# The last unit's second half loaded as one 32 KB part instead of two 16 KB parts

## The chip, the cores and the metric

The kernel runs on one core of a Trainium2 chip. The metric is the device time in microseconds (us), the median of several runs. Before the change it was 780.93 us (780.90 to 780.98, three runs). A profile covers a span that is 1.8 us shorter than the time of the run that it was taken in (779.3 against 781.07 for the kernel before). A transfer is issued by an engine's instruction (SyncE's, for nearly all of those told of here) and waits in that engine's queue for the 16 DMA engines, which carry it in packets; it has landed when the last of the 16 has reported its share.

## The reference

For each of 32 x 128 rows there are four rows of 4096 logits (heads) and four prior logits. Each head goes through a softmax, and the four results are added with the softmax of the priors as weights.

```python
prior_probs = np.exp(prior - prior.max(axis=-1, keepdims=True))
prior_probs = prior_probs / prior_probs.sum(axis=-1, keepdims=True)
softmax = np.exp(logits - logits.max(axis=-1, keepdims=True))
softmax = softmax / softmax.sum(axis=-1, keepdims=True)
mixture = np.sum(prior_probs[..., None] * softmax, axis=2)
```

268.4 MB of logits are read and 67.1 MB are written.

## The kernel before

The rows are cut into 32 units of 128 rows, one row per partition. A unit's four heads are 16 KB each per partition, 2 MB each in all. A tile of two units' logits (`ltile`) is loaded by SyncE's DMA queue; unit u goes into the place of unit u - 2.

```python
def load(u):
    if u == 0 or u >= U - 3:
        cuts = (0, 2, 3, 4) if u == U - 1 else (0, 2, 4)
    else:
        cuts = (0, H)
    for h, to in zip(cuts, cuts[1:]):
        ld = nc.sync.dma_start(
            out=ltile[:, u % 2, h:to], in_=lg[u // J, u % J, :, h:to, :]
        )
        if u >= 2:
            only(ld, adds[u - 2, 0] if h == 0 else exps[u - 2, to - 1])
        else:
            only(ld)
        for k in range(h, to):
            loads[u, k] = ld
```

`only(ins, *keep)` says that the instruction waits for those named and for nothing else. So the part with heads h to `to` waits until unit u - 2 is done with that place, and a head's exponential waits for the load that its head came in.

The loop does, per head, an exponential with a running sum on ScalarE, and then, for all four heads together or, in the last four units, for two at a time (`m` = 4 or 2), a reciprocal on VectorE, a product on GpSimd and the weighted adds on VectorE. The last add of the last unit is done in two halves, each followed by its own store:

```python
for h in range(H):
    ...
    exp(h, *((stores[u - 4],) if late else ()))
    if (h + 1) % m:
        continue
    g = h + 1 - m
    mul = weigh(g, m, *(free if g == 0 else ()))
    for k in range(g, h + 1):
        n = 2 if u == U - 1 and k == H - 1 else 1
        w = V // n
        for c in range(n):
            add(k, mul, c * w, (c + 1) * w)
            if n > 1:
                store(u, acc, nc.sync, c * w, (c + 1) * w)
```

The stores of units 28 to 31 go out on SyncE's queue too, behind the last loads.

The softmax here doesn't subtract the row's maximum and nothing guards it: scores larger than these inputs give would overflow.

## Time and profile before

| what | before | how to read it |
|---|---|---|
| time | 780.93 us | median |
| span of the profile | 779.3 us | first to last instruction of the trace |
| DMA engines | over 90% busy in 39 of 40 slices | the bound |
| VectorE, ScalarE | 67%, 60% busy | not the bound |
| last part of unit 31 lands | 758.96 us | from the trace's landing records |
| half stores of unit 31 issued | 771.19 and 773.45 us | from SyncE's instructions |
| last landing | 778.37 us | 0.91 us before the end of the span |

The lines behind this are shown in the prediction, where they are read. From the list of DMA issues, for the second half store alone (its size, and us from issue to landing):

```profile
out_dram<-ltile SPq DMA_DIRECT2D x1, 1024.0 KB, 4.9
```

### The profile page before, as it was taken

The page shows a single profiled execution, that of the slowest core. Times are in us where ns is not written, and L with a number is a line of the kernel's source. Part 1 is how long each engine was busy: PE and PEld are TensorE (multiplying, and loading weights), DVE is VectorE, ACT ScalarE, POOL GpSimd, SP SyncE. Part 2 cuts the span into 40 slices and gives each one's busy share as a digit, 9 for nine tenths or more (in the row PEclk, how much of TensorE's full clock was granted, in tenths as well). Part 3 has the DMA queues.
Part 4 walks back from the last instruction along what each step waited for, and adds up shares of the span by engine and source line. Part 5 has one row for each costly group of instructions (what it writes and reads, how often), then busy time and mean ns, then how long its engine had stood idle before and what let it go on. Part 6 is the DMA issues. An engine that isn't in the chain of part 4 may idle for free.

```text
span 779.3 us, 654 instructions
## 1 busy us (share of the span) xinstructions
DVE 521.0 (67%) x174; ACT 466.7 (60%) x258; POOL 8.3 (1%) x41
## 2 busy tenths in 40 slices
DVE  4447875558755587555775557855578655689886
ACT  4476555775457755577555675546765567657782
POOL 0000000000000000000000000000000000000000
DMA  9999999999999999999999999999999999999998
GB/s 407 457 417 401 470 407 434 428 461 428 405 467 403 458 420 433 442 443 418 431 454 407 454 408 467 420 415 447 432 442 417 463 399 463 410 427 433 434 429 377
DMA packets 10117, 335.66 MB, mean 431 GB/s; under 512 B 1136, under 2 KB 1136, under 8 KB 1152
## 3 DMA queue, kind: packets, MB, share of 16 engines
q1 hardware_dynamic: 6048, 276.83, 82.3%
q10 hardware_dynamic: 4064, 58.79, 17.6%
q14 instruction: 5, 0.04, 0.0%
HBM read 268.50 MB, written 67.11 MB: 431 GB/s over the span
## 4 chain that ended last, share of the span: by engine, by line
DMA 64%; ACT 27%; DVE 6%; issue 2%; POOL 0%; DVEq 0%; POOLq 0%
DMA ltile<-in_logits_dram 62%; ACT ebuf L159 19%; ACT ltile L159 8%; DVE obuf L177 5%; DMA out_dram<-obuf 2%; DVE ltile L183 1%; POOL coeff L170 0%; DVE rden L168 0%; DVEq L240 0%; POOLq L240 0%; POOLq L170 0%
## 5 line engine op out<-in xcount | busy, mean ns | idle before, releaser
L183 DVE SCALAR_TENSOR_TENSOR obuf<-ebuf,coeff,obuf 128x4096 f32<-128x4096 f32 x90 | 403.6, 4484 | 3.8 <-POOL coeff L170 0.6
L159 ACT ACTIVATE ebuf<-ltile 128x4096 f32<-128x4096 f32 x90 | 322.9, 3589 | 7.4 <-DMA ltile<-in_logits_dram 7.4
L159 ACT ACTIVATE ltile<-ltile 128x4096 f32<-128x4096 f32 x38 | 137.3, 3614 | 280.6 <-DMA ltile<-in_logits_dram 280.6
L168 DVE RECIPROCAL rden<-dsum 128x4 f32<-128x4 f32 (+1 forms) x36 | 6.3, 175 | 227.9 <-ACT ebuf L159 225.1
L177 DVE TENSOR_SCALAR obuf<-ltile,coeff 128x4096 f32<-128x4096 f32 x30 | 70.6, 2353 | 10.2 <-POOL coeff L170 10.2
L183 DVE SCALAR_TENSOR_TENSOR ltile<-ltile,coeff 128x4096 f32<-128x4096 f32 (+1 forms) x7 | 27.0, 3875 | 0.8 <-POOL coeff L170 0.6
L159 ACT ACTIVATION_READ_ACCUMULATOR ebuf<-ltile 128x1 f32 x90 | 16.8, 186 | 0.0
L170 POOL TENSOR_TENSOR coeff<-rden,pp 128x4 f32<-128x4 f32 (+1 forms) x36 | 7.2, 200 | 755.3 <-DVE rden L168 745.4
L159 ACT ACTIVATION_READ_ACCUMULATOR ltile<-ltile 128x1 f32 x38 | 7.1, 186 | 0.0
L139 DVE TENSOR_REDUCE pmax<-pr 16x256 f32<-16x1024 f32 x1 | 1.2, 1208 | 7.8 <-DMA pr<-in_prior_dram 7.8
L141 ACT ACTIVATE pr<-pr 16x1024 f32<-16x1024 f32 x1 | 1.1, 1055 | 7.8 <-DVE pr L140 7.8
L177 DVE TENSOR_SCALAR ltile<-ltile,coeff 128x4096 f32<-128x4096 f32 x2 | 4.7, 2354 | 0.6 <-POOL coeff L170 0.6
L144 DVE TENSOR_TENSOR pn<-pr,pmax 16x1024 f32<-16x1024 f32 x1 | 1.9, 1939 | 0.1
L141 ACT ACT_TABLE_LOAD x1 | 1.3, 1283 | 1.2 <-PEq L229 1.2
L142 DVE TENSOR_REDUCE pmax<-pr 16x256 f32<-16x1024 f32 x1 | 1.2, 1207 | 1.1 <-ACT pr L141 1.1
L149 DVE STREAM_TRANSPOSE pp<-pn 32x256 f32<-32x256 f32 x4 | 1.7, 435 | 0.1
L143 DVE RECIPROCAL pmax<-pmax 16x256 f32<-16x256 f32 x1 | 1.7, 1741 | 0.0
L140 DVE TENSOR_TENSOR pr<-pr,pmax 16x1024 f32<-16x1024 f32 x1 | 1.2, 1211 | 0.0
L138 POOL MEMSET pn<- 32x1024 f32 x1 | 0.9, 941 | 0.3 <-POOLq L229 0.3
L229 POOL MEMSET const-bfloat16-1.0<- 128x1 bf16 x1 | 0.1, 106 | 0.0
L229 POOL MEMSET const-uint8-127<- 128x1 uint8 x1 | 0.1, 106 | 0.0
L229 POOL MEMSET const-float32-0.0<- 128x1 f32 x1 | 0.1, 103 | 0.2 <-issue 0.2
(1 smaller groups left out, 0.1 us busy)
## 6 DMA issues: line engine op xcount, KB each, us to landing
out_dram<-obuf ACTq DMA_DIRECT2D x28, 2048.0 KB, 29.4
ltile<-in_logits_dram SPq DMA_DIRECT2D x7, 4096.0 KB, 26.1
ltile<-in_logits_dram SPq DMA_DIRECT2D x2, 2048.0 KB, 30.9
out_dram<-obuf SPq DMA_DIRECT2D x2, 2048.0 KB, 33.9
out_dram<-ltile SPq DMA_DIRECT2D x1, 2048.0 KB, 17.2
out_dram<-ltile SPq DMA_DIRECT2D x2, 1024.0 KB, 4.8
ltile<-in_logits_dram SPq DMA_DIRECT2D x28, 30.9
pr<-in_prior_dram ACTq DMA_DIRECT2D x1, 64.0 KB, 7.0
```

The costliest lines, as they stand in the source:

```text
L139: nc.vector.reduce_max(pmax, pr, axis=AX.X)
L140: nc.vector.tensor_sub(pr, pr, pmax.unsqueeze(2).to_broadcast([G, R, H]))
L141: nc.scalar.activation(pr, pr, AF.Exp)
L142: nc.vector.reduce_sum(pmax, pr, axis=AX.X)
L143: nc.vector.reciprocal(pmax, pmax)
L144: nc.vector.tensor_mul(pn[0:G].rearrange("g h r -> g r h"), pr, pmax.unsqueeze(2).to_broadcast([G, R, H]))
L149: nc.vector.transpose(pp[32 * t : 32 * (t + 1)], pq[:, :, :, 32 * t : 32 * (t + 1)])
L159: ex = nc.scalar.activation(es[h], lt[:, h], AF.Exp, accum_out=dsum[:, u, h : h + 1])
L168: rc = nc.vector.reciprocal(rden[:, u, h : h + n], dsum[:, u, h : h + n])
L170: mul = nc.gpsimd.tensor_mul(coeff[:, u, h : h + n], rden[:, u, h : h + n], ppu[:, h : h + n])
L177: st = nc.vector.tensor_scalar(out=acc[:, lo:hi], in0=es[h][:, lo:hi], scalar1=coeff[:, u, h : h + 1], scalar2=None, op0=ALU.mult,)
L183: st = nc.vector.scalar_tensor_tensor(out=acc[:, lo:hi], in0=es[h][:, lo:hi], scalar=coeff[:, u, h : h + 1], in1=acc[:, lo:hi], op0=ALU.mu ...
```

## The change

The intent: one DMA fewer, with larger pieces. Head 2 and head 3 of the last unit come as one part.

```diff
     def load(u):
         if u == 0 or u >= U - 3:
-            cuts = (0, 2, 3, 4) if u == U - 1 else (0, 2, 4)
+            cuts = (0, 2, 4)
         else:
             cuts = (0, H)
```

## The prediction

> **What bounds the kernel now.** I read the page first: the busy table, the strip of 40 slices and the chain shares.
>
> ```profile
> span 779.3 us, 654 instructions
> DVE 521.0 (67%) x174; ACT 466.7 (60%) x258; POOL 8.3 (1%) x41
> ...
> DMA  9999999999999999999999999999999999999998
> ...
> DMA 64%; ACT 27%; DVE 6%; issue 2%; POOL 0%; DVEq 0%; POOLq 0%
> ```
>
> VectorE and ScalarE are each busy for only about two thirds of the span, while the 16 DMA engines are over 90% busy in all slices but the last. 335.66 MB at the page's mean of 431 GB/s is 779 us, the whole span. So the kernel is bound by bytes moved, and the change moves none fewer. What it can change is only whether the DMA engines have work in every moment; since it touches the last unit alone, I looked at the end. (A unit is 128 rows; a head of it is 16 KB per row, 2 MB in all.) The table by stretches of time, with columns stretch, its length, busy VectorE, ScalarE and GpSimd, clock, DMA share, GB/s:
>
> ```profile
> 700.00:749.20 49.20, 41.35 (x18) 37.05 (x22) 1.18 (x6) 1.00 1.00 431
> 749.20:759.00 9.80, 9.22 (x4) 9.78 (x5) 0.20 (x1) 1.00 1.01 431
> 759.00:771.20 12.20, 11.82 (x6) 4.72 (x4) 0.20 (x1) 1.00 1.00 430
> 771.20:773.50 2.30, 2.22 (x1) 0.00 (x0) 0.00 (x0) 1.00 0.95 399
> 773.50:779.30 5.80, 0.00 (x0) 0.00 (x0) 0.00 (x0) 1.00 0.63 261
> ```
>
> Even after the last load has landed (about 759) the DMA engines stay full, because stores are queued behind it. Which transfers these are I took from their issues, one at a time (the last column is us from issue to landing), in order of time; the second is the first half of unit 31's store:
>
> ```profile
> ltile<-in_logits_dram SPq DMA_DIRECT2D x1, 2048.0 KB, 31.5
> ```
>
> ```profile
> out_dram<-ltile SPq DMA_DIRECT2D x1, 1024.0 KB, 4.8
> ```
>
> Their issue and landing times, with those of the neighbours read likewise and from the trace's landing records (last of 16 engines): unit 31 heads 0 and 1 land at 749.19, head 2 (issued 723.86) at 754.09, head 3 (issued 727.46) at 758.96; then the stores of units 28, 29 and 30 at 763.85, 768.68 and 773.53; then the two 1 MB halves of unit 31's store, issued 771.19 and 773.45, at 775.95 and 778.37. It is one queue drained without a gap: 4.85 to 4.9 us per 2 MB, 2.42 per 1 MB.
>
> Last the timelines of the two engines in this stretch (start, duration, engine, line, operation):
>
> ```profile
> 749.22 3.62 ACT L159 ACTIVATE ltile<-ltile 128x4096 f32<-128x4096 f32 x1 [2.41 <-DMA ltile<-in_logits_dram]
> ...
> 752.83 3.60 ACT L159 ACTIVATE ltile<-ltile 128x4096 f32<-128x4096 f32 x1
> ...
> 756.43 3.60 ACT L159 ACTIVATE ltile<-ltile 128x4096 f32<-128x4096 f32 x1
> ...
> 760.03 3.60 ACT L159 ACTIVATE ltile<-ltile 128x4096 f32<-128x4096 f32 x1
> ```
>
> ```profile
> 759.42 4.49 DVE L183 SCALAR_TENSOR_TENSOR ltile<-ltile,coeff 128x4096 f32<-128x4096 f32 x1
> 763.82 0.16 DVE L168 RECIPROCAL rden<-dsum 128x2 f32<-128x2 f32 x1
> 764.29 9.13 DVE L183 SCALAR_TENSOR_TENSOR ltile<-ltile,coeff 128x4096 f32<-128x4096 f32 x3 [0.31 <-POOL coeff L170]
> ```
>
> Those are unit 31's four exponentials: they run back to back once 0 and 1 have landed; only the first names a DMA wait. Head 2 landed 2.34 us before its exponential began (756.43 - 754.09), head 3 1.07 us before (760.03 - 758.96). Then the adds of heads 2 and 3 follow, the last in two halves, each followed by a store.
>
> **What the Trainium skill says.** "DMA: Bandwidth & Descriptors", section "Why a DMA increments its semaphore by 16 and not by 1": only the full 16 means that all data has landed, so a consumer of one merged part can't begin on the first head of it. That agrees with the trace here insofar as each load's consumer starts 0.03 us after the last of the 16 landings (749.19, then 749.22). The same page, "Queues, rings and completion order": each engine consumes its ring in order; the landings above are in order of issue. The same page, "Latency and other measured facts", gives about 600 ns as the first-byte latency of such a DMA; here the first half store was issued at 771.19 and its first packets start at 772.02 on seven engines already free, so 0.83 us, and that measurement I use. "ScalarE: Activation LUTs", section "What ACT_TABLE_LOAD costs", gives 186 ns + 0.833 ns per element, 3.6 us for 4096; the trace has 3.60.
>
> **The change, part by part.** It removes one DMA issue of 0.33 us on SyncE (off the path: SyncE waits for its semaphores), and moves another. SyncE's instruction list is one load shorter; the other engines' lists are the same.
>
> Issue: the merged part waits for unit 29's last exponential, so it goes out at 727.46 instead of half at 723.86. Its bytes have their turn in the queue only when the previous part ends, from about 748; 20 us of backlog stand ahead. Cost 0.
>
> Transfer: the same bytes in 32 KB packets instead of 16 KB. In the stretch from 738 to 756 a 16 KB packet takes 612 ns and a 32 KB one 1213, so twice 612 against 1213; by landings, 4 MB in 32 KB packets took 749.19 - 739.47 = 9.72 us and in 16 KB packets 758.96 - 749.19 = 9.77. Gain 0.05 us. The merged part should land at 758.91.
>
> Wait on ScalarE: the exponential of head 2 can't start until then, 758.91 + 0.03 = 758.94 instead of 756.43: 2.51 us later, a new wait of the same length. Head 3's exponential follows it back to back, so it also is 2.51 us later and its own slack (1.07 us) is gone.
>
> VectorE: before, head 3's exponential and its read-out ended at 763.54 + 0.19 = 763.73, and the reciprocal began only at 763.82, since VectorE was finishing the add of head 1. So 0.06 us of the delay is absorbed (0.03 of the 0.09 is the usual hand-over). The adds and the two half stores come 2.45 us later: issues at 773.64 and 775.90 instead of 771.19 and 773.45.
>
> End of the queue: this is where part of the delay is hidden. Before, the first half store was issued ahead of need: unit 30's store kept the slowest engine busy until 773.10, and the first half only landed right behind it. After, with unit 30's store 0.05 us earlier, the queue is empty when the half store is issued. Its packets start at 773.64 + 0.83 = 774.47 on the first engines, and I add 0.2 us for the spread between engines (at the start of the kernel, the first packets of the first load spread from 1.02 to 1.58 us, median 1.15). The two halves then take together what the slowest engine took before, 778.01 - 773.11 = 4.90; the second half, ready at 775.90 + 0.83 = 776.73, is in time to follow the first (774.67 + 2.45 = 777.1). End of packets 779.57, landing 0.36 later as before, 779.93 against 778.37: 1.56 us. So of 2.45 us of delay about 0.9 lies beside the drain of unit 30's store, and some 1.5 is left as a gap in which the DMA engines idle.
>
> Sum: 0 - 0.05 (within the above) + 1.6 = 780.93 + 1.6 = 782.5 us, 0.2% slower.
>
> **The rivals.** First, that it is hidden altogether, because DMA is the bound and ScalarE is far from it: 780.9. The backlog of three stores speaks for it, and it would be so with 1.6 us more of slack at the end: the half store had to be issued by about 773.1 - 0.83 = 772.27 to keep the slowest engine fed, and was issued at 771.19, a slack of 1.1 us against a delay of 2.45. I hold that slack to be too small. Second, that the whole delay reaches the end (783.4), if the half stores take 4.8 us each from issue to landing as now. Against it: the first one's 4.8 us contain queueing behind unit 30's store. For it: a store into an idle queue hasn't been seen in this trace, and its start could be slower than 0.83. Third, that larger packets or one part fewer save time: 780.8. The measured saving is 0.05 us for this part, and it goes into the idle gap rather than to the end. Fourth, that the later issue starves the queue: it would need the 20 us of backlog to be gone by 728, and the 431 GB/s of the first stretch above says no.
>
> **Range and chances.** The mechanism's ends are 1.2 (no spread, or a quicker start) and 2.45 us (nothing hidden), which with 0.1 us of run-to-run spread (before: 780.90 to 780.98) and a small allowance for traffic falling otherwise gives 781.9 to 783.3. For 2% it would need 15.6 us, ten times what is in play; faster or slower by that much is each given 1%.
>
> **What would show it right or wrong.** Right: the last part lands within 0.1 us of 758.9; head 2's exponential names a DMA wait of about 2.5 us; the half stores are issued about 2.45 us later; DMA share falls well under 1 near 773.5 to 774.6; each half store lands 3.5 to 4.3 us after its issue instead of 4.8. Wrong: the exponential of head 2 starts near 756.4; or the span grows by less than 1 us with an unbroken DMA row; or it grows by the full 2.5 us because a store into an idle queue begins later than 0.83 us; or landings anywhere before unit 31 differ by more than run-to-run spread.

## More of the kernel before

All runs told of here are in the fast state, with a granted clock of 1.0.

```profile
q14 instruction: 5, 0.04, 0.0%
```

Five packets of 8 KB in the whole span seem to be nothing. One of them was to matter.

## The result, and the profile after

The changed kernel takes 783.06 us (782.94 to 783.17, six runs) against 780.94 of the kernel before (780.90 to 781.00, six runs): 2.12 us more. Ratios here are the mean time of one kernel's fast runs over that of the other's of the same rounds, so not quite the ratio of the medians quoted; here 1.0027, with an interval from 1.0014 to 1.004. It is within 2%, and inside the predicted range, towards its upper end.

The page after, with the same lines as before:

```profile
span 781.3 us, 652 instructions
DVE 521.1 (67%) x174; ACT 466.8 (60%) x258; POOL 8.4 (1%) x41
...
DMA  9999999999999999999999999999999999999997
```

The work is the same and the DMA row is the same but for its last slice. Two instructions are gone: the load, and a semaphore wait of SyncE that came with it. Next the table by stretches of time of the changed kernel (stretch, length, busy VectorE, ScalarE, GpSimd, clock, DMA share, GB/s):

```profile
749.20:759.00 9.80, 9.21 (x4) 7.40 (x5) 0.20 (x1) 1.00 0.94 406
759.00:771.20 12.20, 9.46 (x5) 7.13 (x4) 0.20 (x1) 1.00 1.00 430
771.20:773.50 2.30, 2.30 (x2) 0.00 (x0) 0.00 (x0) 1.00 0.32 135
773.50:774.60 1.10, 1.10 (x2) 0.00 (x0) 0.00 (x0) 1.00 0.29 119
```

ScalarE is busy for 7.40 us of the first stretch instead of 9.78, so it idles for 2.4. VectorE lacks 2.36 us in the second. The DMA share was 0.95 from 771.2 to 773.5 and is now 0.32: the queue, which was never empty, runs dry before the half stores come.

The timelines of ScalarE and VectorE of the changed kernel (start, duration, engine, line, operation, and in brackets the idle time before it with what ended it):

```profile
749.11 3.62 ACT L159 ACTIVATE ltile<-ltile 128x4096 f32<-128x4096 f32 x1 [2.41 <-DMA ltile<-in_logits_dram]
...
758.82 3.62 ACT L159 ACTIVATE ltile<-ltile 128x4096 f32<-128x4096 f32 x1 [2.40 <-DMA ltile<-in_logits_dram]
...
762.44 3.60 ACT L159 ACTIVATE ltile<-ltile 128x4096 f32<-128x4096 f32 x1
```

```profile
759.32 4.49 DVE L183 SCALAR_TENSOR_TENSOR ltile<-ltile,coeff 128x4096 f32<-128x4096 f32 x1
766.16 0.17 DVE L168 RECIPROCAL rden<-dsum 128x2 f32<-128x2 f32 x1 [2.36 <-ACT ltile L159]
766.64 9.14 DVE L183 SCALAR_TENSOR_TENSOR ltile<-ltile,coeff 128x4096 f32<-128x4096 f32 x3 [0.31 <-POOL coeff L170]
```

Head 2's exponential now waits 2.40 us for the DMA, where before it followed head 1's at once. The wait passes through head 3's exponential to the reciprocal, which now waits 2.36 us for ScalarE, and from there to the adds and stores. (This trace runs 0.1 us ahead of the one before when head 0's exponential starts, 749.11 against 749.22. Where shifts matter they are taken from the landing just before that: 749.09 and 749.19.)

Last the two half stores of the changed kernel, the first and then the second, by size and us from issue to landing:

```profile
out_dram<-ltile SPq DMA_DIRECT2D x1, 1024.0 KB, 3.9
```

```profile
out_dram<-ltile SPq DMA_DIRECT2D x1, 1024.0 KB, 4.5
```

So the time went thus. The half stores are issued 2.46 us later (773.54 - 749.09 = 24.45 against 771.19 - 749.19 = 22.00, before rounding 2.456, and the second likewise). The second one lands 4.49 us after its issue instead of 4.92 (780.29 - 775.80; 778.37 - 773.45), which takes 0.43 back. The end of the span follows the last landing after 0.99 instead of 0.91 us. 2.46 - 0.43 + 0.08 = 2.11 us, against 2.12 in the medians. (The two spans themselves differ by 2.00, since the trace before is already 0.1 us behind at 749 us.)

The mechanism is as predicted. The size is not quite: 1.56 us was forecast. I had expected the second half store to land about 4.0 us after its issue (0.9 us hidden), and it took 4.49. What are those 0.5 us?

### The profile page after: what moved, and what is told of

It reads as the page before. It is cut to its first block, busy times and chain, and to the rows that moved or that the text cites. A ratio compares the mean times of both kernels' runs of the same rounds, so it can differ in the third digit from the quotient of the medians.

```text
span 781.3 us, 652 instructions
## 1 busy us (share of the span) xinstructions
DVE 521.1 (67%) x174; ACT 466.8 (60%) x258; POOL 8.4 (1%) x41
## 4 chain that ended last, share of the span: by engine, by line
DMA 64%; ACT 27%; DVE 6%; issue 2%; POOL 0%; DVEq 0%; POOLq 0%
DMA ltile<-in_logits_dram 62%; ACT ebuf L159 19%; ACT ltile L159 8%; DVE obuf L177 5%; DMA out_dram<-obuf 2%; DVE ltile L183 1%; POOL coeff L170 0%; DVE rden L168 0%; DVEq L240 0%; POOLq L240 0%; POOLq L170 0%
```

## The experiments

Each was timed in five rounds beside the kernel before, which took 780.94 to 780.96 in them. The line numbers of an edited kernel move by the lines added. All twelve runs gave the right result.

### Is it the wait, the later issue, or the larger packets?

**e1_late_issue.** Two parts, but both issued late:

```diff
-                only(ld, adds[u - 2, 0] if h == 0 else exps[u - 2, to - 1])
+                only(ld, adds[u - 2, 0] if h == 0 else exps[u - 2, H - 1])
```

> Before, with the two 16 KB parts kept but the third part issued as late as the merged one (both wait for unit 29's last exponential). My theory (the wait for the merged part costs, the late issue does not, as 20 us of queue stand ahead): as before, 780.9 us within 0.15, head 2's exponential starts without a DMA wait. Rival (the later issue starves the queue): about 783.1.

Measured 781.02 us (780.88 to 781.28). Head 2's part was issued at 727.68 instead of 723.86, and its exponential still followed head 1's without a wait:

```profile
756.64 3.60 ACT L159 ACTIVATE ltile<-ltile 128x4096 f32<-128x4096 f32 x1
```

The later issue costs nothing. The rival of a starved queue is out.

**e2_wait_both.** Two parts issued as before, but head 2's exponential waits for both:

```diff
                 keep = (loads[u, h],) + keep
+                if u == U - 1 and h == 2:
+                    keep += (loads[u, 3],)
```

> Before, with the two 16 KB parts kept and issued as before, but head 2's exponential also waits for head 3's part. My theory (only the moment at which ScalarE may begin counts): as the changed kernel, 783.1 us within 0.2, exponential of head 2 about 2.5 us later than before. Rival (the 32 KB packets or the issue are what costs): 780.9.

Measured 783.38 us (783.32 to 783.50), with the wait there:

```profile
759.00 3.62 ACT L159 ACTIVATE ltile<-ltile 128x4096 f32<-128x4096 f32 x1 [2.54 <-DMA ltile<-in_logits_dram]
```

So the wait alone, with two parts of 16 KB, brings the whole cost. It even costs 0.32 us more than the merged part, just outside what I had allowed. Some of that is that the exponential starts 0.14 us later after head 0's than in the changed kernel (9.85 against 9.71); the rest is explained below.

**e3_merged_weigh_alone and e4_before_weigh_alone.** Heads 2 and 3 of the last unit are weighed one by one, with the merged part and with two parts:

```diff
+                if u == U - 1 and h >= 2:
+                    m = 1
                 if (h + 1) % m:
                     continue
```

> The changed kernel with heads 2 and 3 of the last unit weighed one by one, so that VectorE adds head 2 while ScalarE still does head 3. My theory: VectorE then idles 0.4 us instead of 2.4 before the add of head 2, the first half store goes out only about 0.4 us later than before, inside its slack of 1.1 us, and the time is that of before, 780.9 to 781.2, though the 2.5 us wait on ScalarE is still there. Rival (transfer or issue costs): stays at 783.1.

> The kernel before with heads 2 and 3 of the last unit weighed one by one. My theory (the DMA queue is unbroken to the end, VectorE is not waited for): 780.9 within 0.15, no gain. Rival (the compute path sets the end of before too): a change of the order of the 0.1 to 0.4 us by which the adds move.

With the merged part it measured 781.20 us (781.14 to 781.34): the wait on ScalarE is still there (head 2 starts at 758.72), but VectorE fills it with the add of head 2, and 1.86 of the 2.12 us come back. The timeline of VectorE in that kernel:

```profile
759.21 4.49 DVE L183 SCALAR_TENSOR_TENSOR ltile<-ltile,coeff 128x4096 f32<-128x4096 f32 x1
763.61 0.16 DVE L168 RECIPROCAL rden<-dsum 128x1 f32<-128x1 f32 x1
764.08 4.49 DVE L183 SCALAR_TENSOR_TENSOR ltile<-ltile,coeff 128x4096 f32<-128x4096 f32 x1 [0.31 <-POOL coeff L170]
```

The add of head 2 starts at 764.08 instead of 766.64. So it is VectorE's chain of adds that carries the delay to the end, not the transfer. With two parts it measured 781.37 us (781.35 to 781.47), 0.41 slower, where I had expected nothing. Its half stores are issued 0.33 us later, by the extra reciprocal and product, and its span is 0.18 us longer. So of 0.33 us of delay only 0.15 is hidden: the kernel before has less slack than I thought. The other 0.2 us lie outside the span (in both of these kernels the time is 2.0 us above the span, in the others 1.8), and no view says why; that stays open.

### How much of a delay is hidden?

**e5_delay_0_95, e6_delay_2_5, e7_delay_3_8.** The loads are as before; ahead of the last unit's head 2, ScalarE does 1 x 1024, 3 x 893 or 4 x 1024 elements of needless exponentials:

```diff
+                if u == U - 1 and h == 2:
+                    for _ in range(3):
+                        only(nc.scalar.activation(<pr: 893 elements>, <pn: 893 elements>, AF.Exp),
+                             adds[U - 3, H - 1])
                 exp(h, *((stores[u - 4],) if late else ()))
```

> Before, loads untouched, with one needless exponential of 1024 elements (about 0.95 us) on ScalarE ahead of the last unit's head 2. My theory (a delay is hidden until it uses up the slack of the first half store): half stores 0.9 us later, time 780.9 to 781.1. Rival (every delay of the compute path reaches the end): 781.8.

> Before, loads untouched, with three needless exponentials of 893 elements (about 2.51 us in all) ahead of the last unit's head 2. My theory (the changed kernel's cost is this delay and nothing else): as the changed kernel, 783.0 to 783.2. Rival (part of the 2.1 us is from the transfer): clearly less, such as 782.5 as predicted.

> Before, loads untouched, with four needless exponentials of 1024 elements (about 3.79 us in all) ahead of the last unit's head 2. My theory (past the slack each us of delay costs a us): 1.28 us above the 2.5 us delay, so 784.3 to 784.5. In its trace: do the 16 packets of the two half stores again take 5.0 us and more per engine, and does the last landing again come 0.6 us after the last packet? If these are a property of all engines starting in step, both are as in the changed kernel; if chance, they are not.

Measured 781.80, 783.43 and 785.00 us. All three lie above what was expected. The needless work was a little longer than planned; in e6 it is this, followed by head 2's exponential without a wait for the DMA:

```profile
756.40 2.89 ACT L199 ACTIVATE pr<-pn 16x893 f32<-16x893 f32 x3
759.20 3.60 ACT L159 ACTIVATE ltile<-ltile 128x4096 f32<-128x4096 f32 x1
```

The half stores were issued 0.92, 2.71 and 4.12 us later than before, and the times grew by 0.86, 2.49 and 4.06. My expectation for e5 was wrong: 0.92 us of delay were to be hidden, and all but 0.06 reached the end. That is the rival's figure, 781.8, to the digit. e6 shows that a delay of that size costs what the merged part costs, with the loads untouched; that it exceeds the changed kernel, and the 783.0 to 783.2 expected, fits its longer delay (2.71 against 2.46) and what comes next. From e6 to e7 1.41 us of delay cost 1.57. To the question asked of e7's trace: its engines take about 5.0 us for the two half stores, as in the changed kernel, but the last landing comes 0.48 us after the last packet, not 0.61.

**e8_one_part.** The last unit in one 64 KB part (it also waits for unit 29's last exponential, which the place needs):

```diff
-            cuts = (0, 2, 4)
+            cuts = (0, 2, 4) if u < U - 1 else (0, H)
...
-                only(ld, adds[u - 2, 0] if h == 0 else exps[u - 2, to - 1])
+                only(ld, *((adds[u - 2, 0],) if h == 0 else ()), *((exps[u - 2, to - 1],) if h or u == U - 1 else ()))
```

> The last unit loaded as one 64 KB part. My theory: all four exponentials wait for the last landing, so they begin 9.7 us later and follow at 3.6 us each; the adds end 9.5 us later; less 0.35 us that the drain of the stores hides (as in the changed kernel): 790.0 within 0.4. Rival (a larger part costs in proportion to what it delays in the queue, that is nothing): 781 to 783.

Measured 790.31 us (790.25 to 790.49, four runs). That is within 0.4 of the 790.0 expected: the same reasoning holds at nearly four times the delay (9.46 us at the half stores). The amount taken as hidden was the measured one of the changed kernel, 0.35, so it is no test of that amount; 0.09 is what the medians leave (9.46 against 9.37).

### Where the missing half microsecond went

In e2, e5, e6 and e7 one DMA engine ends its packets 0.5 to 0.6 us after the other fifteen. In those traces the one 8 KB packet of the instruction queue (q14) lies between the two half stores. Around it, on its engine as far as the packets can be followed, three packets of 8 KB take 0.44 to 0.49 us instead of 0.31 (e2 and e6, looked at packet by packet). In e8 it comes after everything, and the last landing is 4.09 us after the last issue. The time of the packet goes with SyncE's place in its program. In the kernels looked at for this (before, changed, e1, e2, e5, e6, e8) its 80th recorded instruction starts 0.6 to 3.1 us before the packet, and merging the two loads took two instructions out of its program. So the packet was taken to be SyncE's own instruction fetch, and the change to have moved it. To test it, instructions were added to SyncE early, where nothing depends on them.

**e9_merged_shift3 and e10_merged_shift1.** The changed kernel with unit 1 loaded in four parts, or in two:

```diff
+        elif u == 1:
+            cuts = (0, 1, 2, 3, 4)      # e10: (0, 2, 4)
         else:
             cuts = (0, H)
```

> The changed kernel with unit 1 loaded in four 16 KB parts, so that SyncE has three DMA issues more, early, where nothing depends on them. Theory A (the 0.5 us by which the changed kernel is slower than predicted is the 8 KB instruction fetch that SyncE's own instruction count puts behind or into the last stores on one DMA engine): the fetch moves ahead of the half stores, the last landing comes about 4.1 us after the last issue instead of 4.49, and the time is about 782.6. Theory B (it is all engines starting in step that makes the tail slow): 783.1 as the changed kernel.

> The changed kernel with unit 1 loaded in two 32 KB parts: SyncE has again as many instructions as in the kernel before. Theory A: the fetch falls between the two half stores, one DMA engine is 0.5 us behind the others, last landing about 4.8 us after the last issue, time about 783.3 to 783.4. Theory B: 783.1.

e9 measured 782.68 us (782.50 to 782.77), 0.38 less than the changed kernel and near the 782.6 that theory A expected, with the same wait and the same delay of the half stores. The fetch was at 760.16. Its second half store, and after it the same of e2 with the fetch in between:

```profile
out_dram<-ltile SPq DMA_DIRECT2D x1, 1024.0 KB, 4.1
```

```profile
out_dram<-ltile SPq DMA_DIRECT2D x1, 1024.0 KB, 4.8
```

And the instruction queue's row of the changed kernel in the stretch from 770 to 790 us, where e9 has no such row:

```profile
q14 instruction: 1, 0.01, 0.1%
```

e10 measured 783.02 us (782.92 to 783.05), not the 783.3 expected. SyncE had 89 recorded instructions, not the 90 that I had counted on, and the fetch stayed behind the second half store (779.75), as in the changed kernel (779.68). So e10 is a second run of the changed kernel's case. The case that it was meant to make, the fetch in between, is shown by e2 and e6, with two parts; with the merged part it was not made.

**e11_before_shift3 and e12_delay_2_5_shift3.** The same edit in the kernel before, and in e6.

> The kernel before with unit 1 loaded in four parts. Theory A: there the two engines that drain the earlier store last set the end and the fetch lies beside them, so 780.9 within 0.2 wherever the fetch goes. Rival (the split of unit 1 itself gains): lower by as much as the run of the changed kernel with the same split is lower than the changed kernel.

> The kernel before with the 2.5 us of needless exponentials and unit 1 loaded in four parts. Theory A: the fetch leaves the half stores, so about 0.6 to 0.7 us less than the 783.4 of the same delay without the split, 782.7 to 782.9. Theory B: 783.4.

e11 measured 781.17 us (781.08 to 781.38), so the split of unit 1 gains nothing by itself; it is 0.23 slower than the kernel before, slightly more than I allowed, though its span is the same to 0.02 us. e12 measured 783.07 us (782.94 to 783.24), 0.36 less than e6 where 0.6 to 0.7 was expected. In its trace the last landing does come 0.70 us sooner after the last issue (4.08 against 4.78), but the end of the span comes 0.10 later after that, and the runs of e6 scatter over 0.25 us. The direction is theory A's, the size of the medians is short of it.

The packets themselves bear this out. In e8, e9, e11 and e12, where the fetch is not among the half stores or right behind them, none of the 256 packets of the half stores takes over 0.35 us. In all the other traces two or three of them take 0.42 to 0.51.

The traces hold two more signs that the fetch is SyncE's. In the six of them in which the 80th instruction finds nothing left to wait for (e1 and e8 to e12), SyncE pauses for 0.42 to 0.43 us just before it, and no other gap from 0.3 to 0.6 us is found between its instructions but one before the very last. So this place in its program is special, though what the pause waits for is not shown. And of the five fetches in the span, those near 148, 194 and 704 us stay within 1.1 us in all fourteen traces, while those at 511 and 775 us move when SyncE's early loads are split (to 487 us in e9 to e12, to 760 in e9 and 742 in e11 and e12; in e10 only the first of the two). In e8 the pause falls behind the last landing, so the end of the span comes 1.45 us after that landing instead of 0.91 to 1.01: the early landing is paid back there.

The readings of the traces together:

| kernel | SyncE instructions | fetch at, us | where that is | last issue to last landing, us |
|---|---|---|---|---|
| before | 90 | 774.85 | between the half stores | 4.92 (behind unit 30's store) |
| e5, e2, e6, e7 | 90 | 775.77 to 778.97 | between | 4.77, 4.78, 4.78, 4.77 |
| changed | 88 | 779.68 | right behind the second | 4.49 |
| e10 | 89 | 779.75 | right behind the second | 4.51 |
| e9 | 93 | 760.16 | before both | 4.10 |
| e12 | 95 | 741.64 | before both | 4.08 |
| e8 | 86 | 788.18 | after everything | 4.09 (but the end comes 0.5 later after it) |

Where the half stores meet an empty queue, three values are found, and the place of the fetch sorts them. With it out of the way 4.1 us; right behind, where the last landing comes 0.61 us after the engine's last packet instead of 0.35, 4.5; in between, 4.8. (In e1, e3, e4 and e11 the half stores are issued before unit 30's store is through, as in the kernel before, and 4.92, 4.61, 4.77 and 5.04 us pass, with the fetch at 777.55, 777.48, 775.18 and 741.71. e5 is at the border: its first packets start while one engine is still busy with unit 30's store.)

## Why the prediction was right or wrong

It was right in the result: within 2%, inside the range, and by the mechanism named. By its steps:

- Issue: cost 0. Right; e1 shows it.
- Transfer: gain 0.05 us. Right: 4 MB took 758.80 - 749.09 = 9.71 us against 9.77.
- Wait on ScalarE: 2.51 us. Right: head 2's exponential started 9.71 us after head 0's instead of 7.21, which is 2.50. e2 shows that the wait alone makes the cost.
- VectorE: 2.45 us at the half stores. Right: 2.46. e3 shows that this is the path by which it reaches the end.
- End of the queue: "So of 2.45 us of delay about 0.9 lies beside the drain of unit 30's store". This term was mis-sized: 0.43. The start was as worked out (first packets 0.83 us after the issue, all engines within 0.15). The failing words are "The two halves then take together what the slowest engine took before, 4.90" and "landing 0.36 later as before". Set to the same landing of heads 0 and 1, the last packet ended about 0.2 us after the forecast and the landing followed it 0.25 later than forecast. With all engines at work at once they took about 5.0 us each, and the slowest, as far as packets can be followed, 5.2 with two slow ones; and SyncE's instruction fetch, which the change itself moved to just behind the second half store, came between the last packet and its landing, 0.61 us later. Take the fetch away and 4.10 us remain (e9), which is 0.82 hidden and 782.68 us, 0.2 above the forecast of 782.5.
- First rival, that it is hidden altogether: rightly thought too small a slack, but the slack of 1.1 us that I gave it was not there. e5 shows 0.06 us of a 0.92 us delay hidden. Its trace lays that to the fetch: fifteen engines end by 778.11, only 0.10 later than the last engine of the kernel before (778.01), and the one with the fetch at 778.67. That a delay of this size without the fetch would be hidden was not run. The kernel before hides its fetch only because two other engines, the last to drain unit 30's store, end later still (at 777.87 and 778.01, by the packets).
- Second rival, that the whole delay reaches the end (783.4): nearly true, though for another reason than a slow start of the store. It is what e2 and e6 measure. By the prediction's own sum this case is 780.93 + 2.45 = 783.38, so the range, which was to hold it, should not have ended at 783.3.
- What would show it: "each half store lands 3.5 to 4.3 us after its issue" held for the first (3.9) and failed for the second (4.5).

A part of the total is luck of the program's length: with one merged load the fetch costs 0.4 us, and with much the same wait and the old number of instructions it costs 0.7 (e2, from issue to landing), which puts e2's 783.38 just outside the predicted range. That the measured time lay inside it was in this sense luck; the wait and its path were not. None of the versions beat the kernel before, whose DMA queue never runs dry.

## What to carry to other kernels

Near the end of a kernel that is bound by its DMA, the size of a part decides when the first consumer may begin, and that counts once the computation behind it feeds the last stores; ask whether those stores still reach a queue that is not empty. An engine with slack on average (VectorE at 67%) can have none in the last 20 us. And before a few tenths of a microsecond are explained by the change, look at which DMA engine ended last and what else it carried.

## What the Trainium skill lacked or had wrong

- "Runtime: NRT & Kernel Launch", section "Instruction fetch mechanics", calls the cost of crossing an instruction block "mostly hidden" and gives blocks of 16 KiB. Here the fetches show as single packets of 8 KB (how large a block is, no run shows), and one that falls among the last stores costs: the last landing comes 4.8 us after the last issue with the fetch in between, 4.5 with it behind, 4.1 without.
- No page says that adding or removing a few instructions on SyncE can move such a fetch into the last stores or out of them. Here it lay at 741.6, 760.2, 774.8, 779.7 and 788.2 us with 95, 93, 90, 88 and 86 recorded SyncE instructions.
- "DMA: Bandwidth & Descriptors", section "Latency and other measured facts", gives about 600 ns to the first byte; the half stores here, issued by SyncE into an empty queue, took 0.83 us from the start of the issue to the first packet, 0.33 of it the issue itself (the page does not say from when it counts).
